# Splitting weight blocks with a casting and an accumulating DMA, in a ring of four slots of two tiles

## The chip, the cores and the metric

The kernel runs on one core of a Trainium2 chip. The metric is the device time of one execution in microseconds (us); the numbers below are the median of three runs, and one execution that was recorded by the hardware profiler.

## What is computed

Four transformer layers for one sequence of 1024 tokens and 1024 features, all in float32. The first is a gated short convolution, the second an attention at three dilations, the third a sparse latent attention that keeps 256 keys per query, the fourth a convolutional feed-forward with 2816 hidden features. The part that matters here is that nearly all of the work is products of activations with weight matrices:

```python
b_gate, c_gate, xin, z = jnp.split(h @ w_in, 4, axis=-1)     # layer 0: 4 x 1024 columns
q, k, v, z = jnp.split(h @ w_in, [...], axis=-1)              # layer 1: 8 x 1024 columns
y = o.reshape(B, S, E).astype(h.dtype) * jax.nn.silu(z)
return y @ w_out
```

## The kernel before

Activations are held feature-major: 128 features on the partitions, 512 tokens (a chunk) along the free axis. A float32 product is made of float32r products, which read rounded operands: an operand is split into `hi`, its value rounded to float32r, and `lo`, the rest, and three matmuls add hi\*hi, hi\*lo and lo\*hi (`gemm`, L339 to L350; all matmuls are recorded at L252).

Weights are laid out in blocks of 128 output columns, 128 partitions x 8 x 128 numbers, 512 KB each. `weight` (L321) brings one: a load by SP's queue into `raw` (L328), a cast on ScalarE into `hi` (L329), a subtraction on GpSimd into `lo` (L330). The three tiles belong to a slot, and there are three slots (`NRING`, L234), used in turn; a slot's `hi` and `lo` are free again when TensorE has done the block's matmuls, its `raw` when GpSimd has done its subtraction.

288 blocks pass through the ring. In layer 0's convolution (`weight0`, `conv_cx`, `conv_zb`) and in layer 1's projections (`block`, L693: seven blocks for each of eight heads) a block is used for both chunks, 48 matmuls. In the out-projections (`outproj`, L614: `w0o`, `w1o`, `w2o`), in layer 2's input (`project`) and in the feed-forward (`ffn_in`: 44 blocks a chunk from `w3i`, `ffn_out`: eight columns of three blocks, 8, 8 and 6 rows deep, from `w3o`) a block serves one chunk, 24 matmuls or 18, and is fetched again for the other chunk.

Other work stands on the same queues. SP's queue carries the modulation weights (`modblock`, L292, 96 loads of 512 KB through a ring of three buffers, L590, in the first 275 us; VectorE multiplies them at L299) and the activations that go by way of DRAM (L624, L939, L1461, L1504). GpSimd's queue carries the keys and values of the sparse attention (L1292, L1293), the second factor and the low part of the rotary embedding (`rotate`, L677 and L686), low parts of activations (L337), and sums of squares (L393). ScalarE's queue carries casts, copies out of PSUM and the Gelu (L1459).

The order of the instructions on each engine's queue is set when the kernel is built, by a scheduler that follows its own estimate of when each instruction can start, with program order as the priority; on the chip each queue runs in that order.

Of the kernel before, what the change touches and what calls it, by code (L numbers as in the profile page):

```python
"""Two blocks of a transformer (a gated short convolution, dilated attention; then sparse latent
attention and a convolutional feed-forward) on one core.

Activations live feature-major: 128 features on the partitions, tokens along the free axis, in
tiles of 512 tokens. A float32 operand of a large product is split exactly into two float32r parts
(hi is the value rounded to float32r, lo the rest), and three passes carry hi*hi + hi*lo + lo*hi.
SBUF is one arena whose pieces are given out and taken back in program order.
"""
# [16 lines left out]
# ---------------------------------------------------------------- layout and constants (host)  # L25
def _blocks(w):
    """(K, N) weight -> (N/128, 128, K/128, 128): one contiguous piece per block of columns."""
    k, n = w.shape
    return np.ascontiguousarray(w.reshape(k // 128, 128, n // 128, 128).transpose(2, 1, 0, 3))


def _cols(v):
    """(n,) vector -> (128, n/128): feature f at partition f % 128."""
    return np.ascontiguousarray(v.reshape(-1, 128).T)
# [81 lines left out]
# ---------------------------------------------------------------- SBUF  # L116
class Arena:
    """Pieces of SBUF, given out and taken back in program order. SBUF is cut into pages; all
    pieces of a page hold either float32 or what float32r products read, and a free page may
    change sides. Of the free runs that are large enough, the one that has been free longest is  # L120
    given, a page changing sides only where the other runs were free for a short time."""

    FRESH = 16
    SMALL = 2  # the first pages are for pieces of at most 288 words

    def __init__(self, pages, make):
        self.make = make  # (page number, words) -> a new tile on that page
        self.words = pages
        self.pages = [[None, None, [(0, n, 0)]] for n in pages]  # rounded?, tile, gaps
        self.clock = 0  # L130
        self.left = self.low = sum(pages)
# [67 lines left out]
# ---------------------------------------------------------------- the program  # L199
def emit(tc, I, OUT):  # L200
# [14 lines left out]
    with sp as sp, pp as pp, dp as dp:  # L215
        serial = [0]

        # the eight banks of PSUM, in rings that are given out in turn
# [15 lines left out]
        NRING = 3  # L234
        wring = []
        for j in range(3):
# [18 lines left out]
        # ------------------------------------------------ constants  # L255
# [29 lines left out]
        def modblock(j, b, ring=None, engine=None):  # L285
            """128 entries of modulation vector j (of 12) as the column mods[:, 8j+b]."""
# [24 lines left out]
        def scale_col(i, gain, j):  # L311
            """scol[i] = gain * (1 + mods[j])."""
# [5 lines left out]
        # ------------------------------------------------ weights  # L318
        wat = [0]

        def weight(src, k=8, m=128, lo_engine=None):  # L321
            """Loads [128, k, m] and splits it, in a slot that lasts for three calls."""
# [3 lines left out]
            raw, hi, lo = (wring[j][i] for j in range(3))  # L326
            v = lambda a: a[:, :n].rearrange("p (k m) -> p k m", k=k)
            dma(v(raw.f), src)  # L328
            A.activation(hi.r[:, :n], raw.f[:, :n], AF.Copy)  # L329
            (lo_engine or G).tensor_sub(lo.r[:, :n], raw.f[:, :n], hi.f[:, :n])  # L330
            return v(hi.r), v(lo.r)

        def split(hi, lo, src, hi_buf_f=None, engine=None):
            """src (AP) -> hi.r, lo.r (Bufs)."""
# [4 lines left out]
        def gemm(w, h, chunks, m=128, tag="mm"):  # L339
            """psum tiles of (w.T @ h) for each chunk; h[k][c] = (hi, lo) Bufs."""  # L340
# [19 lines left out]
        def new2(n=512):  # L360
            return ar.new(n, True), ar.new(n, True)

        # ------------------------------------------------ norms

        def rstd_cols(ssum, dim, n=4):
            """Sums over features of ssum [128, 128 n] -> (mean + eps)^-1/2 as [128 tokens, n]."""
# [9 lines left out]
        def spread(cols, n=4):  # L376
            """[128 tokens, n] -> psum [128, 128 n] with token t's value along every partition."""
# [18 lines left out]
        def norm_apply(x, y, bc, s, b, hi, lo, engine):  # L396
            """(x * bc) * s + b -> hi, lo; y is overwritten (may be x)."""
# [11 lines left out]
        lows = []  # a tile starts when the third one before it is done  # L409
# [8 lines left out]
        def norm_h(xs, acc, s, b, H, c, bc=None):  # L418
            """xs: 8 Bufs of chunk c (freed here); fills H[k][c]."""
# [53 lines left out]
        LOOK = 2  # heads whose queries run ahead in the attention of chunk 0  # L473

        # ================================================ layer 0: gated short convolution
# [18 lines left out]
        held = {}  # weights of the first columns stay until both chunks have used them  # L494
# [119 lines left out]
        def outproj(win, Y, c, gate, xold, xnew, each, apart=()):  # L614
            """x + gate * (w.T @ Y) for chunk c: each(k, xn) gets the new tiles. A generator."""
# [44 lines left out]
        # ================================================ layer 1: dilated attention  # L660
# [11 lines left out]
        def rotate(p, c, out):  # L672
            """Rotary embedding of psum p (tokens of chunk c) into out, a view in token order."""
# [23 lines left out]
        def attend(h, q, k, vs, sz):  # L697
            """q, k: Bufs of the three groups; vs: values in both orders; sz: 2 * silu(z)."""
            st = ar.new(64)
            f = lambda i, n=8: st.f[:, 8 * i:8 * i + 8 * (n // 8)]  # L700
            mx, ng = f(0, 16), f(2, 16)  # maxima and their negatives, group 0 | groups 1, 2
# [906 lines left out]
```

## Time and profile before

| | us |
|---|---|
| median of 3 runs (2806.38 to 2811.24) | 2808.13 |
| span of the profiled execution, first to last instruction | 2805.5 |
| TensorE busy in it | 2606.7 |
| VectorE busy | 1621.9 |
| GpSimd busy | 1366.2 |
| ScalarE busy | 1196.8 |

Only the span is recorded for the profiled execution; it is 2.6 us under the median of the runs. The DMA engines moved 345.16 MB, 123 GB/s over the span. Busy time is an average over stretches that differ: the first 280 us move 209 to 273 GB/s in the slices of the page, the dilated attention between 700 and 1300 us 40 to 65, the feed-forward at the end 72 to 207.

### The profile page before, as it was taken

Reading aid. Unit: us, or ns where it says so; the run is one execution under the profiler, and the core shown is the slowest. Engines: PE = TensorE matmul, PEld = TensorE weight load, DVE = VectorE, ACT = ScalarE, POOL = GpSimd, SP = SyncE. Lnnn points to the kernel's source line nnn. Section 1 sums busy time; section 2 is a strip of 40 time slices with the busy share of each in tenths; the row PEclk is TensorE's granted clock in tenths of the full one; section 3 lists DMA queues with packets and bytes.
Section 4 is the critical chain, followed back from the end, with each engine's and each line's share of the span. In section 5 each row is a group of like instructions: output and inputs, shape, how many; then the busy total and the mean of one; then the engine's idle time right before and its main releaser. Section 6 shows DMA issues by size and latency. Waiting matters only on the chain.

```text
span 2805.5 us, 33530 instructions
## 1 busy us (share of the span) xinstructions
PE 2606.7 (93%) x11942; PEld 2125.5 (76%) x11942; DVE 1621.9 (58%) x3199; ACT 1196.8 (43%) x2028; POOL 1366.2 (49%) x928
## 2 busy tenths in 40 slices
PE   5988999999999999999899778898899989999998
PEld 3866888788888888888777556676787868887787
DVE  8987122403565565566676999998766650343411
ACT  4211223414444454444445667665455542332332
POOL 3323226506535654654476565434544475544453
PEclk9999999999999999999999889899999999999999
DMA  6676115411111111111334533543444643443442
GB/s 257 237 273 209 53 46 180 154 57 61 46 50 65 61 54 46 61 61 40 128 127 143 191 109 118 183 140 122 133 148 137 207 151 107 151 141 135 144 126 72
DMA packets 159140, 345.16 MB, mean 123 GB/s; under 512 B 18386, under 2 KB 58362, under 8 KB 158972
## 3 DMA queue, kind: packets, MB, share of 16 engines
q1 hardware_dynamic: 149612, 317.71, 33.7%
q0 software_dynamic: 9216, 25.17, 3.1%
q8 instruction: 94, 1.54, 0.2%
q14 instruction: 74, 0.61, 0.1%
q10 hardware_dynamic: 144, 0.13, 0.0%
HBM read 285.67 MB, written 58.86 MB: 123 GB/s over the span
## 4 chain that ended last, share of the span: by engine, by line
PE 65%; DVE 19%; DMA 7%; issue 4%; ACT 4%; POOL 2%; SPq 0%; DVEq 0%; POOLq 0%; ACTq 0%
PE p L252 63%; DMA page<-wmod 3%; DVE page L299 3%; DMA page<-d 2%; DVE page L1206 1%; DVE page L1174 1%; DMA d<-page 1%; DVE page L1453 1%; DVE page L1226 1%; POOL wring L330 1%; DVE page L301 1%; DVE page L400 1%; DVE page L1457 1%; PE p L1359 1%; DVE page L1334 1%
## 5 line engine op out<-in xcount | busy, mean ns | idle before, releaser
L252 PE MATMUL p<-page,wring 128*128 128x512 f32 (+2 forms) x8826 | 2092.7, 394 | 75.6 <-ACT page L336 14.8
L252 PEld LDWEIGHTS p<-page,wring 128*128 128x128 f32 (+1 forms) x8826 | 1650.7, 190 | 449.2 <-issue 24.6
L330 POOL TENSOR_TENSOR wring<-wring,wring 128x1024 fp32r<-128x1024 f32 (+1 forms) x288 | 697.0, 2421 | 784.2 <-ACT wring L329 701.9
L252 PE MATMUL p<-page,page 128*128 128x512 f32 (+5 forms) x2444 | 508.5, 350 | 77.0 <-DVE page L379 11.8
L252 PEld LDWEIGHTS p<-page,page 128*128 128x128 f32 (+1 forms) x2444 | 396.5, 195 | 157.1 <-issue 27.6
L329 ACT ACTIVATE wring<-wring 128x1024 fp32r<-128x1024 f32 (+1 forms) x288 | 299.3, 1040 | 405.0 <-PE p L252 374.4
L337 POOL TENSOR_TENSOR page<-page,page 128x512 fp32r<-128x512 f32 (+2 forms) x111 | 172.9, 1563 | 190.0 <-ACT page L336 146.3
L336 ACT ACTIVATE page<-page 128x512 fp32r<-128x512 f32 (+2 forms) x168 | 110.0, 667 | 342.7 <-DMA page<-d 152.9
L677 POOL TENSOR_TENSOR page<-page,page 128x512 f32<-128x512 f32 x96 | 131.1, 1374 | 128.9 <-ACT page L676 128.6
L299 DVE SCALAR_TENSOR_TENSOR page<-page,page 128x1024 f32<-128x1024 f32 x93 | 129.7, 1396 | 31.9 <-DMA page<-wmod 31.5
L679 DVE TENSOR_TENSOR page<-p,page 128x512 f32<-128x512 f32 x96 | 65.2, 684 | 121.4 <-ACT page L676 105.0
L1480 DVE SCALAR_TENSOR_TENSOR page<-p,page,page 128x512 f32<-128x512 f32 (+1 forms) x17 | 12.2, 719 | 203.7 <-PE p L252 203.7
L337 DVE TENSOR_TENSOR page<-page,page 128x512 fp32r<-128x512 f32 (+1 forms) x57 | 66.1, 1170 | 92.4 <-ACT page L336 88.4
L1203 ACT ACTIVATE page<-page,page 128x1024 bf16<-128x1024 f32 (+1 forms) x93 | 86.7, 932 | 63.0 <-DVE page L1226 58.6
L686 POOL TENSOR_TENSOR page<-page,page 128x512 fp32r<-128x512 f32 x64 | 97.3, 1521 | 33.3 <-ACT page L685 33.3
L684 DVE TENSOR_TENSOR page<-page 128x512 f32<-128x512 f32 x64 | 82.3, 1294 | 50.0 <-POOL page L677 50.0
L1453 DVE TENSOR_SCALAR page<-page,page 128x512 f32<-128x512 f32 x44 | 64.5, 1465 | 75.4 <-ACT page L1447 75.4
L675 ACT ACTIVATE page<-p 64x512 f32<-64x512 f32 x96 | 57.2, 596 | 93.0 <-PE p L252 63.5
L685 ACT ACTIVATE page<-page 128x512 fp32r<-128x512 f32 x64 | 56.9, 890 | 71.7 <-DVE page L684 71.3
L1459 ACT ACTIVATE page<-page 128x512 f32<-128x512 f32 x44 | 27.8, 632 | 135.1 <-DVE page L1457 135.0
L625 DVE SCALAR_TENSOR_TENSOR page<-p,page,page 128x512 f32<-128x512 f32 x48 | 35.8, 746 | 84.1 <-PE p L252 84.1
L1206 DVE TENSOR_SCALAR_CACHE_REDUCE page<-page,page 128x768 bf16<-128x768 f32 (+1 forms) x93 | 81.4, 875 | 1.5
(210 smaller groups left out, 2381.4 us busy)
## 6 DMA issues: line engine op xcount, KB each, us to landing
page<-wmod SPq DMA_DIRECT2D x96, 512.0 KB, 4.6
wring<-w3i SPq DMA_DIRECT2D x88, 512.0 KB, 3.7
d<-page SPq DMA_DIRECT2D x137, 256.0 KB, 2.3
page<-d SPq DMA_DIRECT2D x121, 256.0 KB, 3.1
wring<-w1i SPq DMA_DIRECT2D x56, 512.0 KB, 3.6
d<-page SPq DMA_DIRECT2D x32, 512.0 KB, 4.9
page<-d POOLq DMA_DIRECT2D x32, 512.0 KB, 4.7
wring<-w3o SPq DMA_DIRECT2D x32, 512.0 KB, 3.5
```

Source lines behind the costliest of these rows:

```text
L252: lastn["mm"] = T.matmul(out, lhsT=l, rhs=r, start=start, stop=stop)
L299: V.scalar_tensor_tensor(w.f, w.f, 1.0, sil[j // 6].f, op0=OP.mult, op1=OP.mult, accum_out=m)
L329: A.activation(hi.r[:, :n], raw.f[:, :n], AF.Copy)
L330: (lo_engine or G).tensor_sub(lo.r[:, :n], raw.f[:, :n], hi.f[:, :n])
L336: A.activation(hi.r[:, :n], src, AF.Copy)
L337: (engine or V).tensor_sub(lo.r[:, :n], src, hi.f[:, :n])
L677: G.tensor_mul(sw.f, sw.f, rope[1].f[:, CH(c)])
L684: V.tensor_tensor(a.f, a.f, sw.f, op=OP.add)
L686: G.tensor_sub(out[1], shape(a.f), out[2])
L1203: A.activation(junk.b[:, 0:sc.n], sc.f, AF.Sign, scale=-1.0, bias=at, accum_out=one)
L1206: V.tensor_scalar(junk.b[:, 0:sc.n], sc.f, at, None, op0=OP.is_ge, op1=OP.add, accum_out=one)
L1453: V.tensor_scalar(g.f[:, :512], tv(2), kc(2), col("fb")[:, f:f + 1], op0=OP.mult, op1=OP.add)
```

## The change

`weight` no longer uses SP's queue, a `raw` tile or a subtraction. GpSimd's queue issues a load that casts to float32r as it writes `hi`; ScalarE writes the negative of `hi` into `lo`; GpSimd's queue issues a second load of the same block that adds to `lo`, so that `lo` becomes the block less `hi`. A slot is two tiles instead of three, and there are four slots instead of three: 8 x 1024 words of each partition instead of 9 x 1024. The page count of the rest of the SBUF follows from what is left. The diff's other lines remove comments. `weight0`'s first blocks and `weight_own` (L605) keep a `raw` tile and a subtraction of their own.

```diff
-        NRING = 3
+        NRING = 4
         wring = []
-        for j in range(3):
+        for j in range(2):
             t = views(sp.tile([128, 1024 * NRING], F32, name=f"wring{j}"))
             wring.append([Buf(None, None, t, 1024 * i, 1024) for i in range(NRING)])
...
         def weight(src, k=8, m=128, lo_engine=None):
             i = wat[0] % NRING
             wat[0] += 1
             n = k * m
-            raw, hi, lo = (wring[j][i] for j in range(3))
+            hi, lo = (wring[j][i] for j in range(2))
             v = lambda a: a[:, :n].rearrange("p (k m) -> p k m", k=k)
-            dma(v(raw.f), src)
-            A.activation(hi.r[:, :n], raw.f[:, :n], AF.Copy)
-            (lo_engine or G).tensor_sub(lo.r[:, :n], raw.f[:, :n], hi.f[:, :n])
+            G.dma_start(v(hi.r), src)
+            A.activation(lo.r[:, :n], hi.f[:, :n], AF.Copy, scale=-1.0)
+            G.dma_start(v(lo.r), src, accum_op=OP.add)
             return v(hi.r), v(lo.r)
```

## Rows read from the trace of the kernel before

**Rows 1.** The page's first part: busy us of each engine, share, instructions.
```profile
PE 2606.7 (93%) x11942; PEld 2125.5 (76%) x11942; DVE 1621.9 (58%) x3199; ACT 1196.8 (43%) x2028; POOL 1366.2 (49%) x928
```

**Rows 2.** Busy time by stretch: length, PE PEld DVE ACT POOL, PEclk, DMA share, GB/s.
```profile
70.00:264.00 194.00, 174.59 (x721) 140.06 (x720) 161.50 (x284) 35.53 (x53) 52.20 (x23) 0.95 0.71 244
378.00:533.00 155.00, 155.00 (x689) 127.83 (x688) 46.44 (x51) 50.43 (x66) 87.41 (x48) 1.00 0.43 143
705.00:1340.00 635.00, 626.20 (x3183) 526.96 (x3182) 379.94 (x813) 298.73 (x552) 353.08 (x262) 1.00 0.17 56
1413.00:1502.00 89.00, 88.54 (x391) 70.79 (x392) 55.75 (x64) 35.91 (x52) 66.83 (x35) 0.98 0.42 147
2220.00:2760.00 540.00, 522.59 (x2259) 422.75 (x2258) 186.41 (x193) 178.56 (x238) 285.59 (x142) 0.99 0.42 138
```

**Rows 3.** Timeline of `ffn_out`, chunk 0: start, length, what, idle before and releaser.
```profile
2360.51 1.06 ACT L329 ACTIVATE wring<-wring 128x1024 fp32r<-128x1024 f32 x1 [3.08 <-PE p L252]
...
2365.95 1.06 ACT L329 ACTIVATE wring<-wring 128x1024 fp32r<-128x1024 f32 x1 [4.38 <-PE p L252]
...
2370.03 0.85 ACT L329 ACTIVATE wring<-wring 128x768 fp32r<-128x768 f32 x1 [3.02 <-PE p L252]
```

**Rows 4.** Timeline of `ffn_in`, chunk 1: one block's split and matmuls.
```profile
2523.43 1.04 ACT L329 ACTIVATE wring<-wring 128x1024 fp32r<-128x1024 f32 x1
...
2524.56 2.38 POOL L330 TENSOR_TENSOR wring<-wring,wring 128x1024 fp32r<-128x1024 f32 x1 [3.56 <-ACT wring L329]
...
2526.99 5.73 PE L252 MATMUL p<-page,wring 128*128 128x512 f32 x24 [0.21 <-POOL wring L330]
```

**Rows 5.** GpSimd's groups by line: count, busy us, mean ns, idle before.
```profile
L330 POOL TENSOR_TENSOR wring<-wring,wring 128x1024 fp32r<-128x1024 f32 (+1 forms) x288 | 697.0, 2421 | 784.2 <-ACT wring L329 701.9 <-PE p L796 71.8 <-ACT page L769 4.3
...
L1292 POOL DMA_DIRECT2D page<-d x32 | 18.2, 569 | 32.1 <-PE p L252 23.4 <-DVE page L1250 7.2 <-DVE page L1289 1.3
```

**Rows 6.** Waits of all engines: us in total, times, longest us.
```profile
PEld p L252 <- POOL wring L330: 21.7, 25, 2.0
```

**Rows 7.** Timeline at 130 us: the same VectorE multiply before and beside a subtraction.
```profile
128.16 1.22 DVE L299 SCALAR_TENSOR_TENSOR page<-page,page 128x1024 f32<-128x1024 f32 x1
...
130.30 2.67 POOL L330 TENSOR_TENSOR wring<-wring,wring 128x1024 fp32r<-128x1024 f32 x1 [9.70 <-ACT wring L329]
130.63 3.42 DVE L299 SCALAR_TENSOR_TENSOR page<-page,page 128x1024 f32<-128x1024 f32 x1
```

**Rows 8.** Waits of SP's queue.
```profile
SPq L328 <- POOL wring L330: 1068.3, 221, 14.6
```

**Rows 9.** DMA queues: packets, MB, share of 16 engines' span.
```profile
q1 hardware_dynamic: 149612, 317.71, 33.7%
q0 software_dynamic: 9216, 25.17, 3.1%
```

**Rows 10.** DMA issues into the ring, 2220 to 2760 us: count, size, median landing us.
```profile
wring<-w3i SPq DMA_DIRECT2D x44, 512.0 KB, 3.7
wring<-w3o SPq DMA_DIRECT2D x32, 512.0 KB, 3.5
...
wring<-w3o SPq DMA_DIRECT2D x15, 384.0 KB, 3.0
wring<-w2o SPq DMA_DIRECT2D x5, 512.0 KB, 3.9
```

**Rows 11.** DMA issues, 70 to 264 us.
```profile
page<-wmod SPq DMA_DIRECT2D x76, 512.0 KB, 4.4
wring<-w0i SPq DMA_DIRECT2D x12, 512.0 KB, 5.7
```

**Rows 12.** DMA issues from GpSimd's queue, 1990 to 2220 us.
```profile
page<-d POOLq DMA_DIRECT2D x25, 512.0 KB, 5.2
```

**Rows 13.** The same in 2028 to 2036 us, three close together.
```profile
page<-d POOLq DMA_DIRECT2D x3, 512.0 KB, 6.6
```

**Rows 14.** Line 1293's 32 loads from GpSimd's queue, issue to landing.
```profile
DMA to landing us min/median/max: 3.4/4.6/8.4
```

## The prediction

> **What bounds the kernel now.** I read the busy line first: TensorE works 93% of the span [rows 1], so the time is TensorE's work plus some 200 us in which it waits (2805.5 less 2606.7). The table by stretch then says where an edit to the weights can matter. From 378 to 533 us TensorE is never idle, from 1413 to 1502 it idles half a microsecond, from 2220 to 2760 it idles 17 of 540 us [rows 2]. These are the stretches in which a weight block serves one chunk of 512 tokens, 24 matmuls, and is then thrown away: the two out-projections, the second feed-forward half. A block is needed every 5.44 us there, as the steps between two casts released by TensorE show (2360.51 to 2365.95), and every 4.08 us for a block of 768 columns (2365.95 to 2370.03), so 14.96 us for three [rows 3]. In the dilated attention, 705 to 1340 us, a block serves both chunks and is needed half as often.
>
> A block now goes through three places: a load on SP's queue, a cast on ScalarE (1.04 us in [rows 4]), a subtraction on GpSimd (288 of them, 2421 ns each, 697 us together [rows 5]). With three slots it may take two blocks' time after TensorE gives its slot back; cast and subtraction need 1.04 + 2.42 = 3.5 us of 10.9. So the split is nearly hidden: TensorE's weight loads waited for it 25 times, 21.7 us in all [rows 6]. One place where it shows is the feed-forward: ScalarE's cast, queued behind the Gelu, starts at 2523.43, the subtraction follows at 2524.56 and the next matmuls at 2526.99 [rows 4].
>
> **The change, part by part.** I sum against the profiled span, 2805.5 us. The median of the timed runs, 2808.13 us, lies 2.6 us above it; I add changes of the span to the median.
>
> *GpSimd's subtractions go.* That removes 697 us of GpSimd, and brings 2 x 288 DMA issues. An issue of a load from GpSimd's queue takes 569 ns [rows 5], so 328 us come back: 369 us less busy time on an engine that doesn't bound. What it is worth on the path has two pieces. The 21.7 us of waiting for the subtraction end [rows 6]. VectorE is also freed: a multiply of 128x1024 takes 1.22 us alone and 3.42 us where it starts while a subtraction runs [rows 7]. Which of those 2.2 us lie on the path I can't count; in the stretch from 70 to 264 us, where VectorE is busy 161.5 of 194 us [rows 2], I allow four of them, 9 us. Together about -30 us, with bounds of 0 (other waits end last) and -60 (every such overlap counts double).
>
> *SP's queue loses 288 issues*, and with them 1068.3 us in which SP stood still until a subtraction had freed a slot [rows 8]. Loads of activations queued behind them can start earlier; no row shows TensorE waiting for SP for that reason, so 0.
>
> *ScalarE* keeps one operation of the same size and form (a copy, scaled by -1): 0. But it now waits for a DMA where it waited for TensorE, and behind it on ScalarE stand the Gelu and the copies that empty PSUM.
>
> *The transfers.* The loads so far run at 317.71 MB in 33.7% of the span, which is 336 GB/s, and those from GpSimd's queue at 25.17 MB in 3.1%, 289 GB/s [rows 9]. A block of 512 KB therefore occupies the 16 engines for 1.56 us before, and 1.81 us as a load from GpSimd's queue. What a casting load costs no row shows; the nearest one is the plain load from that queue, and I take its 1.81 us, with the queue's slowest case below as the upper end. An accumulating transfer is not in the trace either. It must bring the same 512 KB and also read the 512 KB it adds to: between one load, 1.81 us, and two, 3.62 us. I take it near two, since both operands have to be read. A block then costs 1.81 + (1.81 to 3.62) - 1.56 = 2.1 to 3.9 us more of DMA. From 2220 to 2760 us 96 blocks are fetched (44 + 32 + 15 + 5 [rows 10]) beside a share of 0.42 [rows 2]: 227 us of 540 become 425 to 599 us, 79% to 111%. The Trainium skill bears on which end: Collectives: The Full Stack, Part 3, on why ReduceScatter is half of AllGather, says that the add itself is free and the second source read halves the rate. By that rule the accumulate costs two loads and the upper end holds; without it the lower one would. No transfer in this trace adds, so no row decides.
>
> In the stretch from 70 to 264 us the DMA share is 0.71 already, with 76 loads of modulation weights and 12 of blocks [rows 2, 11]. Twelve blocks add 25 to 47 us of transfers to 194 us, 84% to 95%; the modulation loads, three in flight and 4.4 us each, set VectorE's pace there. I take +25 us, bounds 0 (it fits) and +47.
>
> *The new waits.* This is the term that decides. On GpSimd's queue a block is now two entries: the casting load, which waits until TensorE has given back the slot of four blocks earlier, and the accumulating one, which waits until ScalarE has negated what the first one brought. Queues run in order. If a block's accumulate stands right behind its load, GpSimd is held for the whole first half: landing of the load, ScalarE's 1.04 us with a handover of about 0.1 us (2524.47 to 2524.56 [rows 4]), and the second issue, 0.57 us [rows 5], before the next block's load can be issued at all. Loads of 512 KB from this queue landed after 5.2 us in the median between 1990 and 2220 us [rows 12]. The cycle is 5.2 + 1.04 + 0.1 + 0.57 = 6.9 us a block, against 5.44 and 4.99 us that TensorE needs. The fourth slot doesn't help then, because the limit is one block per turn of the queue.
>
> What that adds: 2220 to 2760 us, 96 x 6.9 = 662 - 540 = 122 us; 1413 to 1502 us, 391 matmuls are 16 blocks, 16 x 6.9 = 110 - 89 = 21 us; the first out-projection, 16 blocks, 110 - 16 x 5.44 = 23 us. Together 166 us, and 8 blocks of the sparse attention's out-projection at 1.46 us, 12 us: +178 us. Bounds: the queue can be arranged so that the next load goes ahead of the accumulate, and then the term is 0 (below nothing it can't go, as TensorE's own 5.44 us stay). With three loads put on this queue close together the median landing was 6.6 us [rows 13], a cycle of 8.3 us: 257 + 44 + 46 = +347 us. With the slowest landing of the trace, 8.4 us [rows 14], it is 10.1 us and +578 us. I take 6.9, nearest to how a block's load meets the accumulate of the block before it.
>
> Behind a waiting entry on GpSimd stand the rotary products and low parts in the dilated attention. GpSimd is busy there 353 of 635 us [rows 2]; seven heads of seven blocks, 49 (the first head's lie before it), lose 49 x 2.42 = 119 us and gain 49 x 1.14 = 56 us of issues and 49 x 6.3 = 309 us of waits: 599 of 635 us, close to full but under it. I take 0 with an upper bound of +50 us, half a head's period.
>
> *The SBUF.* Two tiles of four slots take 1024 words less than three of three, one page more for everything else. Nothing I read waits for a page long enough to price: 0.
>
> **The sum.** 2808 + 178 - 30 + 25 = 2981, so about 2980 us, with 2900 to 3090 as the case's own range (landings of 4.7 to 6 us).
>
> **The rivals.** *A, hidden, on the other side.* The order of GpSimd's queue is planned ahead, and if the load of the next block is put before the accumulate of this one, the queue never holds anything up. A block then needs 5.2 + 1.14 + 5.2 + its issues, 12 to 13 us, and four slots leave three blocks' time, 15.0 to 16.3 us. That is enough as long as the accumulate lands within about 8 us and the DMA share stays at the lower end, 79%. What is left is the relief: 2808 - 30 = 2778, and 2785 with some of the load on the early stretch. For it speaks the slack; against it that waits on GpSimd hit other work too and that the early stretch is near its DMA limit. It decides where the accumulate's landing passes 8 us. 0.2.
>
> *B, the transfers bound.* The queue is well ordered but an accumulate takes two loads' time: 599 us of transfers in 540, +59 us, and 99 of 89 us in the second out-projection, +10; if the engines reach 90%, 125 + 21 = +146 us. With -30 and +25 that is 2872 to 2949, middle 2910. This is where the rule of Collectives: The Full Stack (the Trainium skill, Part 3) would lead. Against it: no long stretch of this trace is above 0.71 [rows 2], so it isn't known where full is. 0.15.
>
> *C, the accumulate is slow and the queue serial.* The next load stands behind an accumulate in the rings and lands after 6.6 us or more: 2808 + 347 - 30 + 47 = 3172, up to 3400 with 8.4 us. 0.22.
>
> *D, no change.* Relief and waits cancel to within 0.2%, 5.6 us, about what a measurement of this kernel can tell from none: 0.07. That the change doesn't do what it says (the load doesn't round, so that the low part is empty) would alter the values, not the transfers, and belongs to whichever case the queue gives.
>
> **How the numbers follow.** Forecast 0.36, A 0.2, B 0.15, C 0.22, D 0.07. Faster is A, 0.2; the same D, 0.07; slower the rest, 0.73. The range from 2785 to 3200 us leaves out about half of A and half of C.
>
> **What would show it.** GpSimd's queue: its issues two to a block, waiting for ScalarE's negation in the forecast and C, for TensorE in A. The steps between blocks in the last feed-forward: 6.9 us in the forecast, 8.3 and above in C, 5.4 in A. DMA share from 2220 us on: near 1 in B, 0.6 to 0.8 otherwise. TensorE's waits there: for a DMA into the ring, which it hardly has now. VectorE's 3.42 us multiplies beside subtractions must vanish in every case. The prediction is wrong if GpSimd's issues of the next block stand ahead of the accumulate and it lands in 5 us (then A), or if an accumulate takes far more than two loads (then beyond C).

## The result, and the profile after

| | before | after |
|---|---|---|
| median of 4 runs each (us) | 2809.52 (2806.38 to 2811.24) | 3027.57 (3023.01 to 3030.13) |
| span of the profiled execution | 2805.5 | 3026.8 |
| TensorE idle in the last stretch (below) | 24.8 | 111.3 |

The changed kernel takes 1.0782 times as long, 95% interval 1.0767 to 1.0796: 218 us more. 2980 us was forecast, with 2900 to 3090 as the case's own range.

The busy line and the two large DMA queues of the profile after answer to [rows 1] and [rows 9]:

```profile
PE 2684.0 (89%) x11942; PEld 2171.4 (72%) x11942; DVE 1374.0 (45%) x3199; ACT 1202.3 (40%) x2033; POOL 1052.6 (35%) x1216
...
q0 software_dynamic: 92160, 322.08, 46.3%
q1 hardware_dynamic: 108140, 169.25, 16.9%
```

GpSimd is 314 us less busy (1366.2 to 1052.6) and VectorE 248 us (1621.9 to 1374.0), as intended. TensorE does the same 11942 matmuls, but is 77 us longer busy with them, and it idles more. The stretch that loses most runs from the last output of the sparse attention to the end of the feed-forward. Busy time by stretch, with the columns of [rows 2]; first of before, then of after, and the two hold the same matmuls (2467 and 2465 of them recorded):

```profile
2220.00:2801.00 581.00, 556.18 (x2467) 452.57 (x2465) 195.36 (x215) 187.06 (x250) 300.18 (x153) 0.99 0.40 132
```

```profile
2313.00:3022.00 709.00, 597.72 (x2465) 477.58 (x2463) 137.19 (x215) 186.32 (x249) 207.38 (x250) 0.93 0.74 180
```

709 against 581 us: 128 us more, of which 86.5 are idle time (709 - 597.7 = 111.3 against 24.8) and 41.5 are longer matmuls, at a mean granted clock of 0.93 where before had 0.99. The DMA engines are at 0.74, not full.

GpSimd's own timeline in `ffn_out`, chunk 1, shows why (start, length, engine and line, what, idle time before and what ended it; L329 is the casting load, L331 the accumulating one, L394 a sum of squares):

```profile
2907.96 0.86 POOL L331 DMA_DIRECT2D wring<-w3o  x1 [6.50 <-ACT wring L330]
2908.55 1.38 POOL L329 DMA_DIRECT2D wring<-w3o  x2
2916.01 1.77 POOL L331 DMA_DIRECT2D wring<-w3o  x2 [6.07 <-ACT wring L330]
2917.32 1.02 POOL L329 DMA_DIRECT2D wring<-w3o  x1
2917.89 1.76 POOL L394 TENSOR_TENSOR page<-page,page 128x512 f32<-128x512 f32 x1
2926.11 0.86 POOL L331 DMA_DIRECT2D wring<-w3o  x1 [6.46 <-ACT wring L330]
```

The pattern repeats every 2926.11 - 2907.96 = 18.15 us, one column of three blocks, where [rows 3] has 14.96. In it GpSimd stands still twice, 6.07 and 6.46 us, each time between a casting load and the accumulate that needs ScalarE's negation of it. Until that accumulate is issued no later load can be. It is one hold for one block, then one hold for two blocks: the fourth slot lets two casting loads go out together.

The waits (engine and line, what they waited for: us in total, times, longest) give the same for the whole program. The first and the third row stand where [rows 8] had SP's 1068.3 us; the second and the fourth are ScalarE waiting for the casting load:

```profile
POOL wring L331 <- ACT wring L330: 976.6, 235, 15.7
...
ACT wring L330 <- DMA wring<-w3i: 252.0, 63, 9.9
POOL wring L329 <- PE p L252: 239.1, 73, 12.8
ACT wring L330 <- DMA wring<-w3o: 196.1, 35, 14.7
```

TensorE now waits for what it hardly waited for before, in its matmuls on weight blocks (busy us, mean ns | idle before, and what ended most of it; the same group idled 75.6 us before, none of it for a DMA into the ring among the first three causes):

```profile
L252 PE MATMUL p<-page,wring 128*128 128x512 f32 (+2 forms) x8826 | 2163.7, 404 | 209.3 <-DMA wring<-w3o 46.2 <-DMA wring<-w3i 42.8 <-ACT page L337 19.5
```

### The profile page after: what moved, and what is told of

Its sections match the earlier page's. It is cut to its first block, busy times and chain, and to the rows that moved or that the text cites. A ratio compares the mean times of both kernels' runs of the same rounds, so it can differ in the third digit from the quotient of the medians.

```text
span 3026.8 us, 33933 instructions
## 1 busy us (share of the span) xinstructions
PE 2684.0 (89%) x11942; PEld 2171.4 (72%) x11942; DVE 1374.0 (45%) x3199; ACT 1202.3 (40%) x2033; POOL 1052.6 (35%) x1216
## 3 DMA queue, kind: packets, MB, share of 16 engines
q0 software_dynamic: 92160, 322.08, 46.3%
## 4 chain that ended last, share of the span: by engine, by line
PE 38%; DMA 22%; issue 19%; DVE 8%; POOL 7%; ACT 5%; SPq 0%; POOLq 0%; ACTq 0%; DVEq 0%
PE p L252 37%; DMA page<-wmod 5%; DMA wring<-w3i 5%; DMA page<-d 2%; DVE page L299 2%; POOL wring L329 2%; POOL wring L331 2%; DMA wring<-w2i 2%; ACT wring L330 1%; DMA wring<-w0o 1%; DMA wring<-w1i 1%; DMA d<-page 1%; POOL page L338 1%; DMA wring<-w2o 1%; DMA wring<-w3o 1%
## 5 line engine op out<-in xcount | busy, mean ns | idle before, releaser
L252 PE MATMUL p<-page,wring 128*128 128x512 f32 (+2 forms) x8826 | 2163.7, 404 | 209.3 <-DMA wring<-w3o 46.2
L252 PEld LDWEIGHTS p<-page,wring 128*128 128x128 f32 (+1 forms) x8826 | 1693.3, 195 | 612.8 <-issue 118.4
L330 ACT ACTIVATE wring<-wring 128x1024 fp32r<-128x1024 f32 (+1 forms) x288 | 299.7, 1044 | 947.6 <-DMA wring<-w3i 252.0
L252 PE MATMUL p<-page,page 128*128 128x512 f32 (+5 forms) x2448 | 515.3, 353 | 105.4 <-DVE page L394 30.2
L338 POOL TENSOR_TENSOR page<-page,page 128x512 fp32r<-128x512 f32 (+2 forms) x111 | 159.8, 1454 | 180.7 <-ACT page L337 178.9
L331 POOL DMA_DIRECT2D wring<-w3i x88 | 79.3, 901 | 348.6 <-ACT wring L330 312.6
L299 DVE SCALAR_TENSOR_TENSOR page<-page,page 128x1024 f32<-128x1024 f32 x93 | 118.7, 1279 | 81.8 <-DMA page<-wmod 81.6
L1454 DVE TENSOR_SCALAR page<-page,page 128x512 f32<-128x512 f32 x44 | 25.0, 568 | 175.5 <-ACT page L1448 175.5
L331 POOL DMA_DIRECT2D wring<-w3o x48 | 42.7, 916 | 173.7 <-ACT wring L330 167.4
L331 POOL DMA_DIRECT2D wring<-w1i x56 | 48.8, 871 | 152.6 <-ACT wring L330 141.2
L338 DVE TENSOR_TENSOR page<-page,page 128x512 fp32r<-128x512 f32 (+1 forms) x57 | 57.5, 1024 | 93.9 <-ACT page L337 89.9
L329 POOL DMA_DIRECT2D wring<-w3i x88 | 65.1, 778 | 48.4 <-PE p L252 42.2
```

The costliest lines, as they stand in the source:

```text
L252: lastn["mm"] = T.matmul(out, lhsT=l, rhs=r, start=start, stop=stop)
L299: V.scalar_tensor_tensor(w.f, w.f, 1.0, sil[j // 6].f, op0=OP.mult, op1=OP.mult, accum_out=m)
L329: G.dma_start(v(hi.r), src)
L330: A.activation(lo.r[:, :n], hi.f[:, :n], AF.Copy, scale=-1.0)
L331: G.dma_start(v(lo.r), src, accum_op=OP.add)
L338: (engine or V).tensor_sub(lo.r[:, :n], src, hi.f[:, :n])
```

## The experiments

To say where a version stands I took, in each trace, the start of the last execution (in the second column the first) of a line that every version runs. The figures are us later (+) or earlier (-) than before at that point, so the difference of two columns is what a stretch cost; lines are those of before.

| version | conv ends (L533) | first rotary embedding (L675) | last rotary embedding (L675) | second out-projection ends (L955) | sparse attention ends (L1363) | `ffn_in` ends (L1447) | `ffn_out` ends (L1480) |
|---|---|---|---|---|---|---|---|
| after | +9.4 | +33.4 | +53.6 | +81.1 | +92.7 | +186.8 | +220.9 |
| e3, no second load | -21.7 | -27.4 | -10.8 | -12.5 | -48.1 | -61.9 | -61.3 |
| e2, second load overwrites | -16.6 | -14.4 | +4.0 | +5.4 | -25.0 | -9.9 | -6.1 |
| e8, accumulate alone | -9.9 | -8.2 | -8.0 | +14.6 | -5.7 | +79.8 | +88.4 |
| e9, casting load alone | -5.3 | +6.4 | +16.7 | +42.4 | +42.0 | +86.3 | +98.2 |
| e12, load ahead of accumulate | -3.2 | -6.9 | +19.7 | +25.6 | +10.4 | +64.3 | +71.5 |
| e15, e12 with overwriting | -23.3 | -28.8 | -8.3 | -10.3 | -47.8 | -49.8 | -49.1 |

My theory was the prediction's: GpSimd's in-order queue is held between the two halves of a block. The rival was that the accumulating transfers themselves are slow, whatever the order.

### e3: without the second load

```diff
             A.activation(lo.r[:, :n], hi.f[:, :n], AF.Copy, scale=-1.0)
-            G.dma_start(v(lo.r), src, accum_op=OP.add)
```

> The second load is left out (lo is only the negative of hi). GpSimd's queue then carries nothing that waits for ScalarE. All theories expect the loss to go; what is left over the time of before, 2809 us, is the price of loading from GpSimd's queue with a cast. Queue theory: 2770 to 2800 us, as the subtractions' 22 us of waits go and nothing takes their place. A theory in which the casting load itself is slow: above 2850 us.

Measured: 2741.9 us, 0.976 of before (0.9745 to 0.9774). GpSimd's waits and the queue of its DMAs:

```profile
POOL wring L329 <- PE p L252: 778.2, 189, 12.7
...
q0 software_dynamic: 50688, 173.63, 21.8%
```

The kernel leaves the block itself out of the low part. Without the second load GpSimd waits for TensorE to give a slot back, so loads go out as early as slots allow. This is what the change would be worth if the low part cost nothing: 67 us, more than twice the relief I had put into the sum, and faster than the 2770 us expected at best. What the second load and its wait cost is therefore about 3028 - 2742 = 286 us; the scheduler also ordered the other engines' instructions anew in e3, and that is in both figures.

### e2: the second load overwrites instead of adding

```diff
-            G.dma_start(v(lo.r), src, accum_op=OP.add)
+            G.dma_start(v(lo.r), src)
```

> The second load overwrites lo where it added to it (lo then holds the whole block); queue, order of issue and waits are the same. Queue theory (GpSimd's in-order queue is held from a block's first load to its negation, so the next load comes late): the first halves are unchanged, the time stays near 3028 us, 2990 to 3035. Transfer theory (the accumulate reads two operands and fills the DMA engines): a block costs 3.6 us of transfers in place of about 4.6, so most of the loss goes, 2840 to 2920 us. If accumulate and overwrite occupy the DMA engines alike, the share of the software queue stays at 46%.

Measured: 2808.0 us, 0.9998 of before (0.9981 to 1.0016). The kernel leaves out the subtraction. The order of the instructions is the changed kernel's on TensorE, VectorE, ScalarE and GpSimd. So a queue order that holds the next load does not by itself cost 218 us, and the queue theory as I had put it fell here; the time is also under the 2840 to 2920 us of the transfer theory. GpSimd's timeline in `ffn_out` tells how the loss went:

```profile
2693.09 0.54 POOL L331 DMA_DIRECT2D wring<-w3o  x1 [5.10 <-ACT wring L330]
...
2694.89 1.31 POOL L394 TENSOR_TENSOR page<-page,page 128x512 f32<-128x512 f32 x1
2701.13 0.57 POOL L331 DMA_DIRECT2D wring<-w3o  x1 [4.93 <-ACT wring L330]
2701.70 1.06 POOL L329 DMA_DIRECT2D wring<-w3o  x2
2708.28 0.54 POOL L331 DMA_DIRECT2D wring<-w3o  x1 [5.51 <-ACT wring L330]
```

The two holds of a column are still there, 4.93 and 5.51 us instead of 6.07 and 6.46. A column takes 2708.28 - 2693.09 = 15.19 us, just over TensorE's own 14.96. So here TensorE hardly notices the holds, and with the adding transfer it does. Of the 18.15 - 15.19 = 2.96 us that it adds to a column, the two holds are 12.53 - 10.44 = 2.09, the sum of squares behind the issues 1.76 - 1.31 = 0.45, and the six issues the remaining 0.42.

The DMA queues price the transfers; GpSimd's queue here:

```profile
q0 software_dynamic: 92160, 322.08, 37.3%
```

It took 46.3% of 3026.8 us after, 37.3% of 2800.3 us here and 21.8% of 2743.5 us in e3, so the second transfer of a block occupied the engines for (1401 - 598) / 288 = 2.79 us when it adds and (1044 - 598) / 288 = 1.55 us when it only writes. The casting load comes to (598 - 87) / 288 = 1.77 us, 87 us being the other loads of that queue (3.1% of 2805.5 us in [rows 9]).

### e12 and e15: the next block's load ahead of the accumulate

The casting load and the negation of the following block are put ahead of a block's accumulate, and the accumulate is tied behind that load on GpSimd's queue. `first_half(a)` holds both instructions for block `a`; the sequence of blocks is listed in the kernel.

```diff
-            G.dma_start(v(hi.r), src)
-            A.activation(lo.r[:, :n], hi.f[:, :n], AF.Copy, scale=-1.0)
-            G.dma_start(v(lo.r), src, accum_op=OP.add)
+            for a in range(j + 1 if j else 0, min(j + 2, len(SEQ))):
+                first_half(a)
+            hi, lo, v, again = halves.pop(j)
+            with tc.issue_after(halves["last"].ins):
+                G.dma_start(v(lo.r), again, accum_op=OP.add)
```

> The changed kernel with one thing different: the order of GpSimd's queue. The casting load of the next block is placed ahead of the accumulating load of this one, by an explicit edge; transfers, waits on data and slots are the same. Queue theory: between 2800 and 2890 us, with steps of 5.4 to 5.6 us a block in the last feed-forward in place of 6.05. Transfer theory: no change, 2980 to 3040 us. Latency theory (two landings in a row don't fit into the slots whatever the order): no better or worse, 3000 to 3100 us, since the accumulate is now issued later.

Measured: 2871.7 us, 1.022 of before (1.0203 to 1.0237), 156 us less than the changed kernel with the same transfers. The edit moved more than GpSimd's queue, as the scheduler ordered every engine anew: compared instruction by instruction, about a fifth of TensorE's matmuls stand elsewhere, most of them in the two attentions, but in the last stretch only a handful of some 2460. The last stretch is therefore the clean comparison, and there e12 loses 61 us (+10.4 to +71.5) where the changed kernel loses 128. GpSimd's timeline in `ffn_out` (L405 casting load, L419 accumulate) and two rows of its waits:

```profile
2770.63 0.55 POOL L405 DMA_DIRECT2D wring<-w3o  x1 [3.14 <-PE p L328]
2771.70 0.85 POOL L419 DMA_DIRECT2D wring<-w3o  x1 [0.52 <-ACT wring L406]
...
2776.08 0.59 POOL L405 DMA_DIRECT2D wring<-w3o  x1 [2.19 <-PE p L328]
2777.09 0.85 POOL L419 DMA_DIRECT2D wring<-w3o  x1 [0.42 <-ACT wring L406]
2780.15 0.55 POOL L405 DMA_DIRECT2D wring<-w3o  x1 [2.21 <-PE p L328]
2781.66 0.86 POOL L419 DMA_DIRECT2D wring<-w3o  x1 [0.95 <-ACT wring L406]
2785.59 0.56 POOL L405 DMA_DIRECT2D wring<-w3o  x1 [3.08 <-PE p L328]
```

```profile
POOL wring L405 <- PE p L328: 611.6, 184, 14.9
...
POOL wring L419 <- ACT wring L406: 276.2, 121, 9.2
```

The waits have changed places: 611.6 us for a free slot and 276.2 us for the negation, where the changed kernel has 239.1 and 976.6. A column takes 2785.59 - 2770.63 = 14.96 us again. That is the prediction's rival A, in this stage to the hundredth. What is left, 62 us in the median and 71 in the profiled execution, lies elsewhere: 54 us between the end of the sparse attention and the end of `ffn_in` (+10.4 to +64.3), and 27 us in the dilated attention (-6.9 to +19.7). In e12 the accumulate lands after 7.6 us in the median of the whole program, close to the 8 us at which I had put A's end, and in chunk 1's `ffn_in` the DMA engines are at 0.86 (columns of [rows 2]):

```profile
2480.00:2730.00 250.00, 221.06 (x917) 178.38 (x916) 60.82 (x102) 70.35 (x94) 65.25 (x84) 0.95 0.86 211
```

So slow transfers, case B's cause, may hold part of what is left; no run separates them from the waits.

The same order with an overwriting second load:

```diff
-                G.dma_start(v(lo.r), again, accum_op=OP.add)
+                G.dma_start(v(lo.r), again)
```

> This kernel keeps the order of e12_ordered (each block's second load behind the next block's casting load) and lets the second load overwrite the low part instead of adding to it, so the low part holds the block itself: it leaves the subtraction out. Theory of two causes (the order of GpSimd's queue and the adding itself): e12's remaining 62 us over the kernel before were the adding transfers; without the add the time falls to 2750 to 2800 us, below e2_plain_second (2808), which kept the changed kernel's order. Rival, that the order was the whole cause and the remaining 62 us are the second set of bytes: near 2870. A second rival, that without an add the order is worth nothing because all holds are short: 2800 to 2810, the same as e2.

Measured: 2760.6 us, 0.9828 (0.9805 to 0.9851). The theory of two causes holds, and it gives a table of four (medians, us):

| | order of the changed kernel | load ahead |
|---|---|---|
| second load adds | 3027.6 | 2871.7 |
| second load overwrites | 2808.0 | 2760.6 |

Of the 267 us between e15 and the changed kernel, 47 come with the order alone, 111 with adding alone, and 108 only where both meet. Between e2 and the changed kernel, and between e15 and e12, the order of the instructions is the same on every engine, so adding is the only difference there. In the last stretch alone, where TensorE's order is all but the same in all four, the table reads +128 and +61 us with adding, +19 and -1 us without. The bytes alone don't make it either: in e15 the same stretch has a DMA share of 0.72, near the 0.74 of the changed kernel, and keeps TensorE fed:

```profile
2172.00:2750.00 578.00, 553.77 (x2461) 455.06 (x2460) 130.02 (x210) 187.09 (x249) 172.53 (x252) 0.98 0.72 222
```

### e14: e12 with the negation done twice

```diff
             A.activation(lo.r[:, :n], hi.f[:, :n], AF.Copy, scale=-1.0)
+            A.activation(lo.r[:, :n], hi.f[:, :n], AF.Copy, scale=-1.0)
```

> e12_ordered's order, with ScalarE's negation done twice: 288 x about 1.05 us, 302 us more on ScalarE, and every low part ready 1.05 us later. If the queue no longer holds a block's load until the negation is done, a later negation costs little: 2870 to 2900 us. If the chain of load, negation and second load of each block still paces the ends, the 96 blocks of 2220 to 2760 us and the 40 of the out-projections lose about 1 us each: 2990 to 3020.

Measured: 2901.3 us, 1.0315 (1.028 to 1.0351), 30 us more than e12 for 288 further negations of 1.05 us, 302 us of ScalarE. It lies 1 us above what the held-queue theory gives and far under the 2990 to 3020 of a chain of load, negation and accumulate that paces the ends. The last stretch loses nothing by it, 46 us where e12 loses 61; the 30 us come before it, and the scheduler's new order is in them. With the load ahead, the negation is mostly out of the way.

### e10: the changed kernel with the negation done twice

The edit of e14, made in the changed kernel.

> The changed kernel with ScalarE's negation done twice (the second writes the same values), which adds 1.05 us between the first load's landing and the accumulate's issue; transfers are the same. Queue theory: two holds for three blocks, 139 one-chunk blocks, 139 x 0.67 x 1.05 = 97 us more, 3090 to 3150 us. Transfer theory: the DMA engines are the limit and have time to wait, 3020 to 3050 us.

Measured: 2955.7 us, 1.0533 (1.051 to 1.0555): 72 us faster than the changed kernel, though each low part is ready 1.05 us later. Neither theory allowed that. What changed with it is the order: the scheduler takes the longer negation into its estimate and places the accumulates later on GpSimd's queue. Counted over the 287 blocks that have a next one, the accumulates that stand ahead of its casting load are

```
after 209   e4 210   e10 129   e12 0
```

and the times are 3028, 3076, 2956 and 2872 us. Between kernels with four slots, fewer such accumulates went with less time. The three points fit the theory, but e10 changes two things at once and shows it less cleanly than e12.

### e8 and e9: one half of the change alone

Both keep three slots of three tiles. e8 keeps SP's load and ScalarE's cast and lets the low part come from a negation and the accumulate; e9 brings `hi` by a casting load from GpSimd's queue, `raw` by SP's, and GpSimd subtracts.

```diff
 e8
             dma(v(raw.f), src)
             A.activation(hi.r[:, :n], raw.f[:, :n], AF.Copy)
-            (lo_engine or G).tensor_sub(lo.r[:, :n], raw.f[:, :n], hi.f[:, :n])
+            A.activation(lo.r[:, :n], hi.f[:, :n], AF.Copy, scale=-1.0)
+            G.dma_start(v(lo.r), src, accum_op=OP.add)
 e9
             dma(v(raw.f), src)
-            A.activation(hi.r[:, :n], raw.f[:, :n], AF.Copy)
+            G.dma_start(v(hi.r), src)
             (lo_engine or G).tensor_sub(lo.r[:, :n], raw.f[:, :n], hi.f[:, :n])
```

> From the kernel before, three slots of three tiles: SP loads raw and ScalarE rounds it into hi as before; only the subtraction is replaced, by a second ScalarE copy (the negative) and an accumulating load from GpSimd's queue. The DMA engines move the same bytes as in the changed kernel. Queue theory: the loads run ahead on SP's queue, a block needs 2 x 1.05 + 6 = 8 us of the 10.9 us that two blocks leave, so 2800 to 2860 us. Transfer theory: same bytes, same loss, 2950 to 3050 us.

> From the kernel before, three slots of three tiles: SP loads raw, GpSimd's queue issues a casting load of the same block into hi in place of ScalarE's cast, and GpSimd subtracts as before. Nothing accumulates. Queue theory: GpSimd is held from the casting load's issue to its landing, about 4 us, and then subtracts for 2.4 us; two such waits for three blocks make 2 x 4 + 3 x 2.4 + 3 x 0.55 + 1.3 = 18 us a column of the last feed-forward in place of 15.0, so 2930 to 3050 us. Theory that only the accumulate costs (its transfers and its landing): 2790 to 2850 us.

Measured: e8 2891.9 us, 1.0295 (1.028 to 1.031), between its two expectations; e9 2903.6 us, 1.0349 (1.0316 to 1.0381). e8 loses nothing until the second out-projection, 23 us there, which layer 2 gives back, and 94 us in the last stretch (-5.7 to +88.4). Its loads go out from SP's queue, so no load is held behind an accumulate; what is long there is a block's chain after TensorE gives its slot back: cast 1.06, negation 1.05, issue 0.88 and landing 6.6 us, 9.6 us and the handovers, against two blocks' time, 9.5 to 10.9 us. e8's stretch, GpSimd's DMA queue and the accumulate's landing (min/median/max) in its trace:

```profile
2214.00:2888.00 674.00, 586.11 (x2459) 472.33 (x2459) 138.02 (x210) 281.51 (x349) 152.14 (x152) 0.93 0.77 188
...
q0 software_dynamic: 50688, 173.63, 32.6%
```

```profile
DMA to landing us min/median/max: 5.0/6.6/14.1
```

These durations alone don't place the loss. TensorE's timeline has most of it, 60 of the 94 us, in chunk 1's `ffn_in`, where it waits some 3 us for a DMA after most pairs of blocks, and next to nothing in chunk 1's `ffn_out`, where two blocks leave the least time:

```profile
2590.49 12.77 PE L252 MATMUL p<-page,wring 128*128 128x512 f32 x48 [3.02 <-DMA wring<-w3i]
2606.19 12.47 PE L252 MATMUL p<-page,wring 128*128 128x512 f32 x48 [2.93 <-DMA wring<-w3i]
...
2779.76 85.10 PE L252 MATMUL p<-page,wring 128*128 128x512 f32 x387
```

In `ffn_in` the second block's cast and negation stand behind the Gelu on ScalarE's queue; whether that makes the difference was not tested.

e9 loses 98 us without a single adding transfer, less than the held queue was expected to cost and more than the rival allows. A casting load and the subtraction that waits for it then stand on one in-order queue, so a hold is possible here too; which of e9's waits ended last I didn't separate.

### e4: three slots

```diff
-        NRING = 4
+        NRING = 3
```

> The changed kernel with three slots of two tiles. If the fourth slot does nothing, as the prediction had it: 3010 to 3050 us. If the fourth slot is what lets two blocks share one hold of GpSimd's queue: each block has a hold of its own, 6.3 + 0.9 + 0.9 = 8 us a block in the one-chunk stretches instead of 6.05, so 3200 to 3350 us.

Measured: 3076.2 us, 1.0961 (1.0943 to 1.098). The fourth slot is worth 49 us to the changed kernel, between the two expectations. With three slots two blocks should less often share a hold, which was not counted; the wait for TensorE to free a slot rises from 239.1 to 381.7 us.

### e13: the subtraction on VectorE at the end

The kernel before, with the low parts of chunk 1's `w3i` blocks and of all `w3o` blocks subtracted on VectorE, which is busy 186 of 540 us there [rows 2].

```diff
-                w = weight(I["w3i"][f])
+                w = weight(I["w3i"][f], lo_engine=V if c else G)
...
-                        accumulate(p, weight(I["w3o"][k][:, a:a + n], n), a, n, whole)
+                        accumulate(p, weight(I["w3o"][k][:, a:a + n], n, lo_engine=V), a, n, whole)
```

> The kernel before, with one difference: in the second chunk's first feed-forward half and in both chunks' second half the low part is subtracted on VectorE (1.2 us) instead of GpSimd (2.4 us). Leaving out all subtractions and the second load made 67 us of difference; if that came from GpSimd's subtraction standing in the way of VectorE and of the matmuls, a part of it comes here: 2775 to 2800 us. If it came from elsewhere (the fourth slot, SP's queue): 2800 to 2815 us, no change.

Measured: 2793.8 us, 0.996 (0.9947 to 0.9973), 12 us or 0.4% under before, the only version with the whole computation that is not slower than before. The gain is one piece: at the start of `ffn_out` it stands 5.7 us behind before, at the end of chunk 1's `ffn_in` 8.1 us ahead.

A casting load from SP's queue, five slots of two tiles and four slots of three were not tried.

## Why the prediction was right, point by point

The direction and the place were right, the mechanism in its main half, and the time fell inside the forecast's own range, 48 us above its middle. That it came so near is in part luck: with e3 as the measure, waits and transfers cost 286 us where the sum has 178 + 25 = 203, and the relief was 67 us where it has 30. By stretch, in us, with e3 beside it to take the relief apart from the waits:

| stretch | predicted | after less before | e3 less before |
|---|---|---|---|
| convolution | +25 | +9.4 | -21.7 |
| first out-projection | +23 | +24.0 | -5.7 |
| dilated attention | 0, up to +50 | +20.2 | +16.6 |
| second out-projection | +21 | +27.5 | -1.7 |
| layer 2 | +12 | +11.6 | -35.6 |
| last stretch | +122 | +128.2 | -13.2 |
| relief, not placed | -30 | | |

The last two columns apart are what the second load cost in a stretch: 31, 30, 4, 29, 47 and 141 us. Layer 2, 47 against 12, and the last stretch, 141 against 122, hold most of the miss; their net figures agree with the forecast only because the relief in them was left out as well.

*The cycle of the held queue* was the deciding term. I had 6.9 us a block: landing 5.2, negation 1.04, handover 0.1, issue 0.57. Measured are 18.15 / 3 = 6.05 us in `ffn_out`, with holds of 6.07 and 6.46 us that are as long as I had them, but two holds for three blocks. So the step that failed is "the fourth slot doesn't help then, because the limit is one block per turn of the queue": the limit can be two blocks per turn, and e4 puts 49 us on it. The last stretch still came out at +128 against +122, because two things were missing from the sum. 41.5 of the 128 us aren't waits but longer matmuls at a lower clock. And many holds in `ffn_in` are longer than those in `ffn_out`, up to 10 us, as in GpSimd's timeline there:

```profile
2723.73 0.91 POOL L331 DMA_DIRECT2D wring<-w3i  x1 [7.03 <-ACT wring L330]
...
2737.07 0.89 POOL L331 DMA_DIRECT2D wring<-w3i  x1 [9.95 <-ACT wring L330]
```

From the start of `ffn_out` to the end of chunk 1's `ffn_in` after loses 186.8 - 110.4 = 76.4 us; eight columns of `ffn_out` by 18.15 - 14.96 = 3.19 us are 25.5 of them, and the 44 blocks of `ffn_in` the other 51.

*That the accumulate sets the hold* was not in the forecast: it took the landing of the casting load, 5.2 us [rows 12], as given by the queue it came from. In e2 the same load in the same order landed after 4.8 us in the median, in the changed kernel after 6.2 (min/median/max of L329, then of L331, after):

```profile
DMA to landing us min/median/max: 3.4/6.2/11.4
```

```profile
DMA to landing us min/median/max: 4.8/5.5/11.3
```

The forecast's 5.2 lies between the two, so the size came out right, by luck, for a mechanism of which half was described. In case C I had the accumulate delay the next load, but as a further loss on top.

*The price of the accumulate*: 2.79 us of the DMA engines against 1.81 to 3.62, and I had taken it near the upper end. The Trainium skill (Collectives: The Full Stack, Part 3) says of a collective's reduction that the second source read halves the rate; here an adding transfer took 2.79 / 1.55 = 1.8 times the plain one of the same place. The 2.79 us hold the assumption that the casting load costs what it does in e3; e8, whose accumulates have no casting load beside them, gives (943 - 87) / 288 = 2.97 us, 1.9 times. Case B nevertheless didn't come: the last stretch is at 0.74 of the DMA engines. The casting load at 1.77 us against 1.81 was right.

*The relief* was mis-sized: -30, bounds 0 and -60, against the 67 us that e3 gains (the fourth slot, the freed SP queue and a new order are in these). VectorE's multiply of line 1453 alone went from 1465 to 568 ns. I had counted only overlaps in the first 264 us; e3 gains 36 us of it in layer 2.

*The dilated attention* cost 20 us where I had 0 with a bound of 50. It isn't the hold: e3, which has no accumulate, shows 16.6 there, e12 26.6, and e8, whose loads are on SP's queue, 0.2. So it comes with the casting load on GpSimd's queue among the rotary products. Which of these products it delays was not tested.

*The early stretch*: VectorE's waits for modulation weights rose from 31.5 to 81.6 us and the last of these multiplies came 31 us late, near the +25; but only 9 us of it reached the end of the convolution. In e2 and e15 that multiply is 6 and 5 us late, so most of this comes with the adding, not with the bytes.

*The fourth slot's space and SP's queue*, both put at 0: no run separates them.

*Two slips in the working.* The low end of the range doesn't follow from its landing: 4.7 us give a cycle of 6.4 us and a sum of 2915 us, not 2900. And of the three loads of [rows 13] "close together" the third goes out 4.8 us after the second. Neither moves the forecast.

*What was to be seen*: GpSimd's issues wait for the negation, as in the forecast; DMA share 0.74, inside its 0.6 to 0.8; TensorE waits for DMAs into the ring. The 6.9 us step was 6.05. And VectorE's slow multiplies did not all vanish: one of line 299 still takes 3.24 us, and GpSimd still has subtractions of its own (111 at line 338).

## What to carry to other kernels

If an engine's in-order queue issues both a load and a second step that waits for that load's result, everything behind the second step waits for the landing. Look in the trace at which of the two, the second step or the next load, stands first; here putting the next load first gave back 156 of 218 us.

An operation taken off a busy engine that did not set the end is paid with whatever replaces it. Here 697 us of subtractions were hidden but for some 67 us, and the transfers that replaced them were not.

A cycle that stays within its consumer's is free, and one that goes over it costs the excess every turn: in `ffn_out` the holds of 5 us cost 0.2 us a column and those of 6.3 us cost 3. Price such a term with the landing that the changed traffic will have, not with the one it has now.

## What the runs showed of the hardware

An accumulating transfer is longer at its issue too. An issue of L331 took 0.88 us in the median where the overwriting one in e2 took 0.53, and the casting load that follows it took 0.85 instead of 0.54. Duration in ns, min/median/max, for the feed-forward's weights in the changed kernel and in e2:

```profile
L329 POOL DMA_DIRECT2D wring<-w3i x88: 532/856/1134, 1901.7 to 2832.8; - x88
...
L331 POOL DMA_DIRECT2D wring<-w3i x88: 849/884/1352, 1911.8 to 2842.2; - x88
```

```profile
L329 POOL DMA_DIRECT2D wring<-w3i x88: 527/537/857, 1808.9 to 2638.2; - x88
...
L331 POOL DMA_DIRECT2D wring<-w3i x88: 527/530/820, 1816.8 to 2646.2; - x88
```

In e12, where the casting load doesn't stand right behind an accumulate, its median is 0.58 us, so the longer record goes with standing behind one. These records overlap: in the first timeline above the next instruction starts 0.59 us after an accumulate of 0.86 us. So little of it reaches the queue, the 0.42 us a column worked out at e2. The queue's bytes are the same with and without adding (322.08 MB in both): what the add reads of its target isn't counted, only the time shows it.

Short stalls of TensorE can cost more than their length. In `ffn_out` after, TensorE idled 2.54 us for a DMA, and the matmuls that followed took 6.64 / 21 = 316 ns instead of 14.40 / 61 = 236 ns (TensorE's timeline, then busy time in windows of 4 us with the granted clock in the third column from the right):

```profile
2904.71 14.40 PE L252 MATMUL p<-page,wring 128*128 128x512 f32 x61
2921.65 6.64 PE L252 MATMUL p<-page,wring 128*128 128x512 f32 x21 [2.54 <-DMA wring<-w3o]
```

```profile
2917.00:2921.00 4.00, 2.11 (x10) 1.42 (x8) 0.00 (x0) 0.72 (x1) 2.65 (x3) 1.00 0.89 143
2921.00:2925.00 4.00, 3.35 (x11) 2.71 (x12) 0.00 (x0) 0.24 (x1) 0.00 (x0) 0.75 0.81 217
2925.00:2929.00 4.00, 4.00 (x16) 3.27 (x15) 0.00 (x0) 0.81 (x1) 1.98 (x3) 0.82 0.36 38
2929.00:2933.00 4.00, 4.00 (x19) 3.30 (x19) 0.36 (x1) 0.04 (x1) 0.00 (x0) 1.00 1.06 305
```

Right after the stall the granted clock is 0.75 and then 0.82, means over windows in which it stood at the lower of its two levels, 1.2 GHz, for part of the time, and then it is at 2.4 GHz again. Not every stall is followed by that: after one of 2.47 us in the next columns the clock stayed up.

```profile
2958.50 9.78 PE L252 MATMUL p<-page,wring 128*128 128x512 f32 x42 [2.47 <-DMA wring<-w3o]
...
2958.50:2962.50 4.00, 4.00 (x18) 3.31 (x19) 0.00 (x0) 0.72 (x1) 0.00 (x0) 1.00 0.66 190
```

Over the program the mean clock went from 0.971 to 0.947 and TensorE's busy time from 2606.7 to 2684.0 us with the same matmuls. 77 of the 221 us by which the span grew are such longer matmuls.
